# Matmul with RMS norm: one row block transposed by DMA instead of TensorE, with the products around it in a new order

## The chip, the cores and the metric

The kernel runs on one core of a Trainium2 chip. The metric is the device time in microseconds (us) of one execution, as the median of several runs. Engines are named as in the profile: PE is TensorE's matmul, PEld its weight load, DVE is VectorE, ACT is ScalarE, POOL is GpSimd, SP is SyncE (here only a queue that issues DMAs).

## The reference

All arrays are float32; a and b are 2048 x 2048, gamma has 2048 elements.

```python
x = np.matmul(a, b)
rms = np.sqrt(np.mean(x ** 2, axis=-1, keepdims=True) + eps)
return (gamma * x / rms).astype(np.float32)
```

## The kernel before

**Blocks and products.** The 16 blocks of 128 rows of a are taken in pairs, "groups" g (`NG = 8`). For a pair (rows r and r+1 of blocks) and a half j of b's columns, the 2x2 product of quarters is made by Strassen's scheme in Winograd's form: seven products m = 1..7 instead of eight, each of 8 matmuls (kp = 0..7) of 128x128 by 128x512, into one PSUM bank of 512 columns. `product_matmul(g, j, m, bank, kp, start)` (L353) issues one of them, `product` (L364) all eight. The stationary side is a quarter of transposed a (`quarter`, L321) or one of four sums of quarters (`sum_of`, `a_sums`, L331), the moving side a quarter of b or a sum (`b_diff`, `b_rest`). Sums s1, s2, s3, s4 of a feed products 5, 6, 7 and 3. A product's bank is often copied into another by ACT and the next product added on top, so the order of products and of copies is fixed by the banks: eight in all, `tbank` and `acc[0]` to `acc[6]`.

**Stages.** Blocks 0 to 3 are the head (`HB = 4`): they are computed while b arrives, the left half in `stream`, the right half in `stream_right` (L476), where blocks 0 and 1 go by plain matmuls (`head_matmul`, banks `acc[0:4]` called `plain`) and the pair of blocks 2 and 3 (`PAIR`) by products, in banks `u2`, `u4`, `p7` = `acc[4:7]`. Lines 519 to 566 end the pair and prepare blocks 4 and 5. Then `first_segment` (L611) and `segment(n)` (L642) work off the halves n = 0, 1, 2, ...: n = 0 and 1 are the left and right half of blocks 4 and 5 (group 2), n = 2 and 3 those of blocks 6 and 7, and so on. `do(n, m)` (L576) is product m of half n with the copies that follow it, `take(n, what)` (L595) brings a finished quarter into the output rows in SBUF.

**Preparing a block.** A block of a is loaded as float32 (`load_block`, L132, issued on POOL's queue), ACT sums its squares (`row_norm`, L223: two passes of 1024 columns and a root), DVE makes a scale out of it (`row_factor`, L233: four small instructions), multiplies the block by it into fp16 (`row_apply`, L244, all 2048 columns in one instruction, or two of 1024 in `prepare`, L248), and the result is transposed. Blocks 4 and 5 are transposed on TensorE: `transpose_half` (L194) is eight 128x128 transposes into one PSUM bank, and `take_transposed` (L204) copies that bank to SBUF. Blocks 6 and up use `prepare`, whose two halves go through `nc.sync.dma_start_transpose` on SP's queue.

**Finishing a row.** `square_half` and `square_right` (L278, L299) sum squares of an output row on ACT, the latter with the root; `finish(mb, order)` (L309) takes the reciprocal on DVE, multiplies each half by it and gamma (one instruction of 1024 columns) and stores it by a DMA on SP's queue. Output rows share eight slots of SBUF (`slot_of`, L256): block 4's left half goes to the slot of block 0's left half, block 5's left half to that of block 0's right half, block 4's right half to that of block 1's left half. A slot can be written only when the store of its earlier owner has read it.

**What sets the order.** The schedule is manual: every engine and every queue works strictly in the order of the program, and semaphores are put in for the data. `wait_for(src)` (L145) is a tiny POOL copy that holds POOL's queue, and so the loads behind it, until src is there. The loads of blocks 4 and 5 follow b's on the queue; those of blocks 6, 7 and 8 are three `load_block` calls at L515, L541 and L557, and block 9 comes in segment 1 behind `wait_for` on transposed block 7. Float32 blocks 4, 6, 9 share one buffer, 5 and 7 the other, block 8 has its own.

**The places that matter below**, in program order: L521 (ACT copies `u2` out), L528 (product 6 of the pair), L529 (DVE copies `u2` to `u4`), L536 and L537 (products 3 and 5 of the pair), L538 (transposes of block 4), L552 to L556 (product 4 of the pair with the transposes of block 5 in it), L558 (sums of group 2), L611 to L634 (half 0), and in `segment(1)`: `square_right(r2)`, `finish(r2, (1, 0))` and then

```python
        if j == 1:
            if first:
                a_two_sums(g)
            a_sums(g + 1, (1, 2))
```

whose sum s2 is the stationary side of `do(2, 6)`, the first product of segment 2.

Of the kernel before, what the change touches and what calls it, by code (L numbers as in the profile page):

```python
# [17 lines left out]
def kernel(  # L18
# [13 lines left out]
    nc = tc.nc  # L32
# [10 lines left out]
    HB = 4  # L43
# [224 lines left out]
    def x_chunk(mb, c):  # L268
        return x_tile(mb, c // 2)[:, (c % 2) * CH:(c % 2 + 1) * CH]
# [206 lines left out]
    def stream_right(kp):  # L476
# [11 lines left out]
        if kp == KP - 1:  # L488
            product_matmul(PAIR, 1, 7, p7, kp - 1, True)
        product_matmul(PAIR, 1, 2, u4, kp, True)  # L490
# [4 lines left out]

    for kp in range(KP):
# [22 lines left out]
    r2, r3 = HB - 2, HB - 1  # L519
    x11, x12, x21, x22 = (x_chunk(r, c) for r in (r2, r3) for c in (2, 3))  # L520
    copy_on("A")(out=x11, in_=u2)  # L521
# [6 lines left out]
    product(PAIR, 1, 6, u2, start=False)  # L528
# [5 lines left out]
    row_apply(HB + 1)  # L534
    evict(plain[2:3], "A")
    product(PAIR, 1, 3, acc[0])  # L536
    product(PAIR, 1, 5, u4, start=False)  # L537
    turned = [transpose_half(HB, h, (tbank, acc[1])[h]) for h in range(2)]  # L538
    take_transposed(HB, 0, turned[0], nc.scalar.copy)
    take_transposed(HB, 1, turned[1], nc.vector.tensor_copy)  # L540
    load_block(HB + 3)  # L541
    for r in range(HB):
        take_pre(r)
    square_right(0)
    evict(plain[3:], "A")
    square_right(1)

    def turn(h):
        view = transpose_half(HB + 1, h, (tbank, acc[2])[h])
        take_transposed(HB + 1, h, view, nc.vector.tensor_copy)  # L550

    for kp in range(KP):  # L552
        if kp == 6:
            turn(0)
        product_matmul(PAIR, 1, 4, u2, kp, False)
    turn(1)  # L556
    load_block(HB + 4)  # L557
    a_sums(G0, (3, 1, 2), False)  # L558

    def pair_ends():  # L560
        nc.scalar.copy(out=x22, in_=p7)
        nc.scalar.copy(out=x12, in_=u4)
        add(x21, u2, x22)
        add(x22, x12, x22)
        add(x12, acc[0], x12)
# [4 lines left out]
    B1, B2, B3, B7 = (acc[1], acc[0]), acc[3:5], (acc[6], acc[5]), acc[2]  # L570

# [4 lines left out]
    def do(n, m, copies=True):  # L576
# [4 lines left out]
        b1, b2, b3 = B1[n % 2], B2[n % 2], B3[n % 2]  # L581
# [13 lines left out]
    def take(n, what, engine="A"):  # L595

        x11, x12, x21, x22 = chunks(n)
        if what == 11:
            copy_on(engine)(out=x11, in_=B1[n % 2])
# [11 lines left out]
    def first_segment():  # L611
        n, g, j = 0, G0, 0
        nxt = 2 * g + 2
        do(n, 1)
        do(n, 7, False)
        finish(0, (1,))
        pair_ends()
        do(n, 2)
        row_norm(nxt)
        a_sums(g, (4,))  # L620
        finish(0, (0,))
        do(n, 6)
        do(n + 1, 1)
        prepare(nxt)
        do(n, 5)
        nc.scalar.copy(out=chunks(n)[2], in_=B7)
        take(n, 22)
        row_norm(nxt + 1)
        take(n, 11)
        finish(1)  # L630
        do(n, 4)
        take(n, 21)
        prepare(nxt + 1)
# [8 lines left out]
    def segment(n):  # L642
# [7 lines left out]
        do(n, 6)  # L650
# [25 lines left out]
        if g < G2:  # L676
            do(n, 2)
            take(n, 11)
# [233 lines left out]
```

## Time and profile before

| what | value |
|---|---|
| time, median of 3 runs | 219.43 us (219.11, 219.43, 220.07) |
| profiled execution, its time | 218.97 us |
| its span (first to last instruction) | 217.2 us |
| mean granted clock of TensorE | 0.995 |
| busy PE / DVE / ACT / POOL | 207.3 / 161.4 / 113.1 / 35.6 us |
| HBM read / written | 34.60 / 16.78 MB |
| TensorE transposes of blocks 4 and 5 (L198) | 32, from 63.19 to 66.87 us |
| DMA transposes (L253) | 20, of 128 x 1024 fp16 each |

Times are positions in the span or lengths, in us. A line of the timeline is: start, length, engine, line of the kernel, operation, what is written and read (output first), shapes, count, and in brackets the idle time of the engine just before and what ended it. Matmuls are pipelined: each is shown as 0.379 us long, but they start 0.2157 us apart (eight in 1.73 us), and it is the distance of starts that counts on PE. The chain of waits lists the pieces of work that followed on each other up to the end. "To landing" is the time from a DMA's issue to its completion.

### The profile page before, as it was taken

The numbers are of one execution on the slowest core, as the hardware profiler recorded it, in microseconds if no ns is written. First come the engines' busy times: TensorE is split into PE (matmuls) and PEld (weight loads), VectorE is DVE, ScalarE is ACT, GpSimd is POOL, SyncE is SP. The second block draws the span as 40 slices with busy tenths as digits, with TensorE's granted clock in tenths as the row PEclk, the third lists the DMA queues.
The fourth block names the chain that finished last, engine by engine and source line by source line (L and its number), as shares of the span: only waits on it lengthen the run. The fifth ranks groups of instructions, "written<-read, shape, count | busy, mean of one in ns | idle before, by whom it ended". The sixth has DMA issues, their size and how long they took to land.

```text
span 217.2 us, 2953 instructions
## 1 busy us (share of the span) xinstructions
PE 207.3 (95%) x1000; PEld 97.2 (45%) x1020; DVE 161.4 (74%) x323; ACT 113.1 (52%) x222; POOL 35.6 (16%) x74
## 2 busy tenths in 40 slices
PE   7999999999999999999999999999999999999960
PEld 3544544444455444444444444444444444444420
DVE  1128869999899997788975899399859883385771
ACT  2110002900599569498626962585777651555771
POOL 7554444334001000100021001102010000000020
PEclk9999999999999999999999999999999999999997
DMA  7999999999959798978674975499985960040455
GB/s 152 168 202 210 201 204 210 212 206 213 405 202 382 290 263 229 330 295 241 162 239 172 340 246 96 187 237 271 278 307 153 284 218 0 0 193 3 193 191 195
DMA packets 37040, 46.60 MB, mean 215 GB/s; under 512 B 22561, under 2 KB 26657, under 8 KB 35745
## 3 DMA queue, kind: packets, MB, share of 16 engines
q0 software_dynamic: 10608, 23.86, 44.8%
q1 hardware_dynamic: 26144, 22.29, 33.9%
q10 hardware_dynamic: 272, 0.26, 0.3%
q8 instruction: 8, 0.13, 0.2%
q14 instruction: 8, 0.06, 0.1%
HBM read 34.60 MB, written 16.78 MB: 237 GB/s over the span
## 4 chain that ended last, share of the span: by engine, by line
PE 68%; DMA 23%; DVE 2%; POOL 2%; issue 2%; ACT 1%; ACTq 0%; DVEq 0%; POOLq 0%
PE acc L361 61%; DMA b<-in_b_dram 18%; DMA early<-in_a_dram 5%; PE acc L400 3%; PE tbank L400 2%; POOL b L115 1%; DVE early L101 1%; PE tbank L361 1%; POOL early L119 1%; ACT a L779 1%; PE acc L198 0%; PE tbank L198 0%; DVE acc L529 0%; DVE x L101 0%; DVE b L101 0%
## 5 line engine op out<-in xcount | busy, mean ns | idle before, releaser
L361 PEld LDWEIGHTS <-s 128*128 128x128 f16 (+1 forms) x312 | 30.5, 98 | 36.9 <-DVE s L338 0.3
L275 ACT ACTIVATE sq<-x 128x1024 bf16<-128x1024 f32 (+1 forms) x33 | 33.2, 1005 | 22.6 <-DVE x L101 18.8
L409 PE MATMUL acc<-b,head_at 128*128 128x512 bf16 x171 | 42.1, 379 | 0.2
L314 DVE SCALAR_TENSOR_TENSOR x<-x,r,gamma_sb 128x1024 f32<-128x1024 f32 x28 | 35.0, 1282 | 0.5
L361 PE MATMUL acc<-b,head_at 128*128 128x512 bf16 x135 | 33.9, 379 | 0.2
L101 DVE TENSOR_TENSOR x<-acc,x 128x512 f32<-128x512 f32 x33 | 22.2, 686 | 12.5 <-PE acc L361 6.7
L361 PEld LDWEIGHTS <-head_at 128*128 128x128 f16 (+1 forms) x192 | 18.7, 98 | 22.2
L361 PE MATMUL acc<-b,at_even 128*128 128x512 bf16 x110 | 26.2, 379 | 0.1
L361 PE MATMUL acc<-early,s 128*128 128x512 bf16 x100 | 25.3, 379 | 0.2
L409 PEld LDWEIGHTS <-head_at 128*128 128x128 bf16 x176 | 16.9, 98 | 19.1
L361 PE MATMUL acc<-b,s 128*128 128x512 bf16 x102 | 24.1, 379 | 0.2
L227 ACT ACTIVATE sq<-a 128x1024 bf16<-128x1024 f32 x22 | 23.3, 1058 | 1.7 <-DMA a<-in_a_dram 1.4
L361 PEld LDWEIGHTS <-at_even 128*128 128x128 f16 x160 | 15.6, 98 | 18.6
L361 PE MATMUL acc<-t_left,s 128*128 128x512 bf16 x93 | 22.2, 379 | 0.1
L115 POOL DMA_DIRECT2D b<-in_b_dram x32 | 17.2, 540 | 20.5 <-DMA b<-in_b_dram 13.8
L448 ACT COPY x<-acc 128x512 f32<-128x512 f32 x7 | 4.0, 581 | 25.3 <-PE acc L409 25.3
L591 ACT COPY acc<-acc 128x512 f32<-128x512 f32 x12 | 6.9, 575 | 10.4 <-PE acc L361 10.4
L190 DVE COPY head_at<-tbank 128x1024 bf16<-128x1024 bf16 x7 | 4.8, 693 | 7.5 <-PE tbank L185 7.5
L296 DVE RECIPROCAL r<-rms 128x1 f32<-128x1 f32 x16 | 2.5, 159 | 9.7 <-ACT rms L291 9.7
L101 DVE TENSOR_TENSOR x<-tbank,x 128x512 f32<-128x512 f32 x9 | 6.2, 690 | 4.2 <-PE tbank L438 4.1
L782 POOL TENSOR_SCALAR x<-x,r 128x512 f32<-128x512 f32 x2 | 1.4, 688 | 47.8 <-DVE r L296 47.8
L593 ACT COPY x<-acc 128x512 f32<-128x512 f32 x10 | 5.8, 584 | 5.3 <-PE acc L361 4.9
(129 smaller groups left out, 243.4 us busy)
## 6 DMA issues: line engine op xcount, KB each, us to landing
out_dram<-x SPq DMA_DIRECT2D x29, 512.0 KB, 3.0
a<-in_a_dram POOLq DMA_DIRECT2D x9, 1024.0 KB, 6.0
b<-in_b_dram POOLq DMA_DIRECT2D x32, 256.0 KB, 9.9
a<-in_a_dram POOLq DMA_DIRECT2D x4, 512.0 KB, 9.8
early<-in_a_dram POOLq DMA_DIRECT2D x7, 256.0 KB, 10.0
gamma_sb<-in_gamma_dram POOLq DMA_DIRECT2D x2, 512.0 KB, 9.8
head_at<-in_a_dram POOLq DMA_DIRECT2D x1, 1024.0 KB, 7.8
out_dram<-x SPq DMA_DIRECT2D x3, 256.0 KB, 2.6
```

Of the source, the lines that this page charges most:

```text
L101: nc.vector.tensor_tensor(out=out, in0=in0, in1=in1, op=op)
L115: nc.gpsimd.dma_start(out=raw[j][kp][:, t, :], in_=b[lo:lo + P, j * HALF:(j + 1) * HALF])
L190: nc.vector.tensor_copy(out=head_at[:, 2 * kp:2 * kp + 2, :, :], in_=view)
L227: nc.scalar.activation(out=junk, in_=a32[mb][:, h * HALF:(h + 1) * HALF], func=ACTF.Square, scale=2.0 ** -8, accum_out=n2[:, h:h + 1])
L275: nc.scalar.activation(out=sq[:, 0:src.shape[-1]], in_=src, func=ACTF.Square, scale=inv_sqrt_n, accum_out=msq[mb][:, c:c + 1])
L314: nc.vector.scalar_tensor_tensor(out=x, in0=x, scalar=inverse_of[mb], in1=gamma_sb[:, h * HALF:(h + 1) * HALF], op0=ALU.mult, op1=ALU.mult)
L361: nc.tensor.matmul(bank, lhsT[:, kp, :], rhs, start=(start and kp == 0), stop=(kp == KP - 1), skip_group_check=not start)
L400: nc.tensor.matmul(bank, lhsT[:, k, :], rhs, start=(m in (1, 7) and k == 0), stop=(k == KQ - 1), skip_group_check=m not in (1, 7))
L409: nc.tensor.matmul(bank, head_at[:, kt, r, :], head_rhs(c, kt), start=(kt == 0), stop=(kt == KT - 1))
L448: copy_on(engine)(out=x_chunk(*g), in_=banks[g])
L591: nc.scalar.copy(out=b3, in_=b2)
L593: nc.scalar.copy(out=chunks(n)[2], in_=B7)
```

## The change

- Block 5 is no longer transposed on TensorE. DVE multiplies it into fp16 in two halves, and SP issues a DMA transpose for each. The 16 transposes and the two DVE copies out of PSUM go.
- In the last step of `stream_right`, ACT's copy of `u2` and the first four matmuls of the pair's product 6 stand ahead of the pair's product 2; the other four stay where product 6 was.
- The pair's products 3, 5, 4 are split: 3 (four matmuls), 5, 4 (six), transposes of block 4, 4 (two), 3 (two), and the last two of product 3 later in `first_segment`. The sums at the end of the pair are arranged anew; bank `acc[2]` is emptied by DVE, later, instead of ACT.
- `first_segment` takes products 1 of half 0 and half 1, then products 2 of both (half 1 in `tbank`), the rest of the pair's product 3, then 7, 6 of half 0, 6 of half 1, 5, 4. Products 1, 2 and 6 of half 1 are so taken out of `segment(1)`. `finish` of block 0's left half, the sums s4, `finish` of block 1 and `take(0, 21)` move; `prepare(7)` now stands ahead of `take(0, 21)`.
- The load of block 7 waits on POOL for block 6 to have landed; the load of block 8 waits for transposed block 6.

```diff
--- before.py
+++ after.py
@@ -486,13 +486,18 @@
         for g, kt in first:
             head_matmul(banks[g], *g, kt)
         if kp == KP - 1:
+            copy_on("A")(out=x11, in_=u2)
             product_matmul(PAIR, 1, 7, p7, kp - 1, True)
+            for k in range(4):
+                product_matmul(PAIR, 1, 6, u2, k, False)
         product_matmul(PAIR, 1, 2, u4, kp, True)
         if kp < KP - 1:
             product_matmul(PAIR, 1, 7, p7, kp - 1, True)
         for g, kt in second:
             head_matmul(banks[g], *g, kt)

+    r2, r3 = HB - 2, HB - 1
+    x11, x12, x21, x22 = (x_chunk(r, c) for r in (r2, r3) for c in (2, 3))
     for kp in range(KP):
         load_later(1)
         b_diff(1, kp)
@@ -516,58 +521,56 @@

-    r2, r3 = HB - 2, HB - 1
-    x11, x12, x21, x22 = (x_chunk(r, c) for r in (r2, r3) for c in (2, 3))
-    copy_on("A")(out=x11, in_=u2)
     product_matmul(PAIR, 1, 7, p7, KP - 1, True)
     b_rest(1, KP - 1)
     add(x11, u4, x11)
     evict(plain[:1], "A")
     row_norm(HB)
     row_norm(HB + 1)
-    product(PAIR, 1, 6, u2, start=False)
+    for kp in range(4, KP):
+        product_matmul(PAIR, 1, 6, u2, kp, False)
     nc.vector.tensor_copy(out=u4, in_=u2)
     row_factor(HB)
     row_apply(HB)
     evict(plain[1:2], "D")
     row_factor(HB + 1)
-    row_apply(HB + 1)
-    evict(plain[2:3], "A")
-    product(PAIR, 1, 3, acc[0])
-    product(PAIR, 1, 5, u4, start=False)
+
+    def part(m, bank, lo, hi, start=False):
+        for kp in range(lo, hi):
+            product_matmul(PAIR, 1, m, bank, kp, start)
+
+    part(3, acc[0], 0, 4, True)
+    part(5, u4, 0, KP)
+    part(4, u2, 0, 6)
     turned = [transpose_half(HB, h, (tbank, acc[1])[h]) for h in range(2)]
     take_transposed(HB, 0, turned[0], nc.scalar.copy)
     take_transposed(HB, 1, turned[1], nc.vector.tensor_copy)
+    src, f = a32.pop(HB + 1), factor.pop(HB + 1)
+    for h in range(2):
+        half = slice(h * HALF, (h + 1) * HALF)
+        nc.vector.tensor_scalar_mul(out=a16_first[:, half], in0=src[:, half], scalar1=f)
+        nc.sync.dma_start_transpose(at(HB + 1)[:, h * KP:(h + 1) * KP, :], a16_first[:, half])
+    wait_for(a32[HB + 2][:, 0:1])
     load_block(HB + 3)
     for r in range(HB):
         take_pre(r)
-    square_right(0)
+    part(4, u2, 6, KP)
+    part(3, acc[0], 4, 6, True)
+    nc.scalar.copy(out=x21, in_=p7)
+    nc.scalar.copy(out=x12, in_=u4)
     evict(plain[3:], "A")
-    square_right(1)
-
-    def turn(h):
-        view = transpose_half(HB + 1, h, (tbank, acc[2])[h])
-        take_transposed(HB + 1, h, view, nc.vector.tensor_copy)
-
-    for kp in range(KP):
-        if kp == 6:
-            turn(0)
-        product_matmul(PAIR, 1, 4, u2, kp, False)
-    turn(1)
-    load_block(HB + 4)
-    a_sums(G0, (3, 1, 2), False)
-
-    def pair_ends():
-        nc.scalar.copy(out=x22, in_=p7)
-        nc.scalar.copy(out=x12, in_=u4)
-        add(x21, u2, x22)
-        add(x22, x12, x22)
-        add(x12, acc[0], x12)
+    add(x22, x12, x21)
+    add(x21, u2, x21)
+    evict(plain[2:3], "D")
+    x12_pair = x12

     halves = [(g, j) for g in range(G0, NG) for j in range(2)]
     B1, B2, B3, B7 = (acc[1], acc[0]), acc[3:5], (acc[6], acc[5]), acc[2]
+
+    def b1_of(n):
+        return tbank if n == 1 else B1[n % 2]

     def chunks(n):
         g, j = halves[n]
@@ -578,7 +581,7 @@
         if n >= len(halves) or n < 0:
             return
         g, j = halves[n]
-        b1, b2, b3 = B1[n % 2], B2[n % 2], B3[n % 2]
+        b1, b2, b3 = b1_of(n), B2[n % 2], B3[n % 2]
         if g >= G2:
             b1 = b2
         product(g, j, m, {1: b1, 2: b1, 3: b3, 4: b2, 5: b3, 6: b2, 7: B7}[m],
@@ -596,7 +599,7 @@

         x11, x12, x21, x22 = chunks(n)
         if what == 11:
-            copy_on(engine)(out=x11, in_=B1[n % 2])
+            copy_on(engine)(out=x11, in_=b1_of(n))
         elif what == 12:
             copy_on(engine)(out=x12, in_=B3[n % 2])
         elif what == 22:
@@ -612,25 +615,34 @@
         n, g, j = 0, G0, 0
         nxt = 2 * g + 2
         do(n, 1)
+        square_right(0)
+        do(n + 1, 1)
+        square_right(1)
+        do(n, 2)
+        do(n + 1, 2)
+        part(3, acc[0], 6, KP, True)
+        finish(0, (1,))
+        a_sums(g, (3, 1, 2), False)
         do(n, 7, False)
-        finish(0, (1,))
-        pair_ends()
-        do(n, 2)
         row_norm(nxt)
-        a_sums(g, (4,))
+        prepare(nxt)
+        add(x12_pair, acc[0], x12_pair)
         finish(0, (0,))
         do(n, 6)
-        do(n + 1, 1)
-        prepare(nxt)
+        load_after(at(nxt)[:, KT - 1, 0:1], HB + 4)
+        product(g, 1, 6, B2[1], False)
         do(n, 5)
         nc.scalar.copy(out=chunks(n)[2], in_=B7)
+        finish(1, (0,))
+        a_sums(g, (4,))
         take(n, 22)
         row_norm(nxt + 1)
+        nc.scalar.copy(out=B3[1], in_=B2[1])
         take(n, 11)
-        finish(1)
+        prepare(nxt + 1)
         do(n, 4)
         take(n, 21)
-        prepare(nxt + 1)
+        finish(1, (1,))
         square_half(2 * g + 1, j)

     X2, W2, Y2 = tbank, B1[1], B1[0]
@@ -647,7 +659,8 @@
             block_segment(n)
             return
         first = g >= G2 and (g - G2) % 2 == 0
-        do(n, 6)
+        if n > 1:
+            do(n, 6)
         own = nxt + (g == NG - 2)
         if j == 0:
             finish(ra - 1)
@@ -673,13 +686,15 @@
                 b_two(4)
             elif not first and g > G2:
                 finish(ra - 2)
-        if g < G2:
+        if g < G2 and n > 1:
             do(n, 2)
             take(n, 11)
         if g == G2 - 1 and j == 1:
             b_two(3)
             b_two(1)
         do(n + 1, 1)
+        if n == 1:
+            take(n, 11)
         if j == 1 and g + 2 < NG:
             wait_for(at(nxt + 1)[:, KT - 1, 0:1])
             if G0 < g < NG - 3:
```

## The prediction

> **What bounds the kernel now.** I read the page's busy shares and slices first, then the chain of waits, then the timeline of the stretch that changes, then the DMA issues.
>
> ```profile
> PE 207.3 (95%) x1000; PEld 97.2 (45%) x1020; DVE 161.4 (74%) x323; ACT 113.1 (52%) x222; POOL 35.6 (16%) x74
> ...
> PE   7999999999999999999999999999999999999960
> ```
>
> PE is full from the second slice to the last but two. In the stretch of 60 to 91 us it is busy for 30.79 of 31. So only fewer PE instructions save time, and anything that makes PE wait costs its whole length. The chain of waits around the change:
>
> ```profile
> 60.02 0.70 DVE acc L529
> ...
> 61.20 0.23 DVE msq L240
> ...
> 61.47 1.89 PE acc L361 x8
> 63.35 0.45 PE tbank L198 x8
> 63.80 0.45 PE acc L198 x8
> 64.25 1.29 PE acc L361 x6
> 65.54 0.45 PE tbank L198 x8
> 65.99 0.43 PE acc L361 x2
> 66.42 0.45 PE acc L198 x8
> ```
>
> The last two L198 rows are block 5's transposes: 0.45 + 0.45 us. The DVE rows ahead say that DVE is close behind PE here. The timeline shows how close the next tight place is:
>
> ```profile
> 80.52 0.68 DVE L101 TENSOR_TENSOR x<-acc,x 128x512 f32<-128x512 f32 x1
> ...
> 81.23 1.06 ACT L275 ACTIVATE sq<-x 128x1024 bf16<-128x1024 f32 x1 [1.59 <-DVE x L101]
> ...
> 83.98 0.29 ACT L291 ACTIVATE rms<-msq,pre 128x1 f32<-128x1 f32 x1
> ...
> 84.31 0.16 DVE L296 RECIPROCAL r<-rms 128x1 f32<-128x1 f32 x1 [0.96 <-ACT rms L291]
> 84.50 2.48 DVE L314 SCALAR_TENSOR_TENSOR x<-x,r,gamma_sb 128x1024 f32<-128x1024 f32 x2
> ...
> 87.27 0.69 DVE L338 TENSOR_TENSOR head_at<-head_at 128x1024 f16<-128x1024 f16 x1 [0.28 <-DMA head_at<-a]
> 88.05 0.69 DVE L338 TENSOR_TENSOR s<-head_at 128x1024 f16<-128x1024 f16 x1
> ...
> 90.88 1.89 PE L361 MATMUL acc<-t_left,s 128*128 128x512 bf16 x8
> ```
>
> Read it as one rope: `take(0, 21)` on DVE (80.52) lets ACT square block 5's left half (81.23) and then block 2's right half; its root (83.98) lets DVE finish block 2 (84.31, 84.50); then come sums s1 and s2 of group 3 (87.27, 88.05). `do(2, 6)` needs s2, done at 88.74, and starts at 90.88: 2.1 us of slack. Last, the DMA transposes: those of block 7, beside no load (first fence), and a later pair issued 1.4 us after a load was (second).
>
> ```profile
> L253 SPq DMA_TRANSPOSE head_at<-a_half x1: 1238/1238/1238, 82.6 to 82.6; - x1
> L253 SPq DMA_TRANSPOSE head_at<-a x1: 1243/1243/1243, 84.0 to 84.0; - x1
> ...
> DMA to landing us min/median/max: 3.1/3.2/3.3
> ```
>
> ```profile
> L253 SPq DMA_TRANSPOSE at_even<-a_half x1: 1238/1238/1238, 151.3 to 151.3; - x1
> L253 SPq DMA_TRANSPOSE at_even<-a x1: 3215/3215/3215, 152.7 to 152.7; - x1
> ...
> DMA to landing us min/median/max: 5.3/5.5/5.8
> ```
>
> **The change part by part.** The sum is made against the profiled execution, 218.97 us (span 217.2 and 1.77 around it); the median of the runs is 0.46 higher, and I add the difference to the median. Positions below are in the span. A matmul takes 0.2157 us on PE, a product 1.726.
>
> *Removed:* 16 transposes, 0.90 us of PE with nothing beside them, so -0.90. The two DVE copies out of PSUM (0.69 each) go too, and DVE's one multiply of 1.28 becomes two of 0.74 (rows of L252).
>
> *Moved to the front:* four matmuls of product 6, issued from 56.72. They wait for ACT's copy of `u2`, which as before can start at 55.84 and takes 0.59: done 56.43, no wait. The four second head matmuls move 0.87 later (4 x 0.2157), and with them ACT's copy of `plain[0]` (57.35 to 58.22) and the back-to-back chain of both `row_norm` behind it: block 4's root ends at 61.37 instead of 60.50, block 5's at 63.91.
>
> *Products 3, 5, 4 of the pair:* product 5 now starts after only four matmuls, at 60.60, but needs `u4`, which DVE writes until 60.72 as before (it is bound by the end of product 6). With 0.05 to pass it on: +0.17. Product 5 then ends at 62.50, six matmuls of product 4 at 63.79. Block 4's scaled copy: root 61.37, four small DVE instructions, multiply from 62.20 to 63.48: just in time for the transposes at 63.79, cost 0; the bank of their second half is emptied by 64.07, used at 64.24. They end at 64.69; two and two matmuls fill up to 65.56. `do(0, 1)` needs that second half copied out of its own bank: DVE starts 64.89, ends 65.58, so PE starts at 65.72: +0.16.
>
> *Block 5's DMA transposes.* DVE multiplies from 65.50 and 66.28, SP issues at 66.32 and 67.76 (1.44 apart, as at 76.52 and 77.96); SP's queue is empty there. Landing 3.1 us after the second at best: 70.9. The load of block 6 is issued 0.87 later than before (64.03, as DVE frees its buffer later) and takes 5.1, so it is in flight beside them. Upper bound by the pair at 151: 67.76 + 5.8 = 73.6. I take 71.6, because here the load has a start of 2.3 us instead of 1.4. DVE is busy until 71.2 with block 0's right half (root on ACT at 69.72); s3 then ends at 72.3. `do(0, 7)`, behind four products and two matmuls, comes at 73.06. Cost 0, with 0.7 of slack; beyond a landing at 72.3 every late microsecond is one of PE.
>
> The Trainium skill (DMA: Bandwidth & Descriptors, DMA Transpose (X-bar), Alternative transpose paths) calls TensorE's way useful when the data is already on the chip, as it is here: that rule speaks against the move, and followed it would leave the 0.90 us in place and the sum at no gain. Its section Rules for kernel authors says that a transpose beside ordinary DMAs needs nothing; that is about correctness, and by it as a rule of time the landing would be 70.9 and never bind, where the row at 151 shows 5.3 to 5.8.
>
> *ACT and DVE in half 0.* ACT from 67.65 without a gap: copy, block 0's right squares and root, copy (69.63), block 1's (70.23), then `row_norm(6)` from 71.61, root done 74.28 (durations of rows 66.13 to 68.20 and 70.07 to 72.74). Before, that root was done at 72.74, and DVE never waited for it. DVE, idle from about 73.8, starts `prepare(6)` at 74.40. From there it is full: `prepare` 2.32 (75.00 to 77.32 before), the pair's add 0.61, two halves of `finish` with a reciprocal 2.59, s4 0.62, `take(0, 22)` 0.61 at 80.54, `prepare(7)` 81.15 to 83.47, and only then `take(0, 21)`, done 84.15 instead of 81.20. `do(0, 3)` needs s4 (80.64) and `take(0, 22)` (81.24), and comes at 81.70: 0.
>
> *The queues.* POOL: the load of block 7 waits for block 6 (about 69.3) and is issued near 70, landing 76.1 by the median of 6.1, used by ACT at 77.8: 0. The load of block 8 waits for transposed block 6 (80.5) and goes out near 81.2; ACT wants it after 94: 0 for itself, but it now flies beside block 7's transposes (82.67 and 84.10), so by the row at 151 those land at 89.4 instead of 87.2. Block 9's load waits for them: 90 instead of 87.8, used after 100. SP: block 0's left half is stored behind block 6's transposes, at 78.8 instead of 75.1, landing 81.7 (2.9; at worst 4.6, 83.4); ACT's `take(0, 11)` writes that slot and must be done for `do(2, 1)` at 83.43: 82.4, cost 0; at worst 84.0, cost 0.6.
>
> *The rope.* ACT squares block 5 at 84.20 (after `take(0, 21)`); block 2's root ends, with the rows' spacing, at 86.87. DVE: reciprocal 86.97, two halves of `finish` 87.16 to 89.64, s1 89.6 (block 7 landed 89.4, just no wait), s2 done 91.1. PE reaches `do(2, 6)` at 73.06 + 10 products = 90.32 and starts at 91.2: +0.9. ACT's copy into its bank ends at 90.53, less than that. Bounds: 0 if DVE's rope is 0.9 shorter than I count, 1.4 if block 7 lands half a microsecond later.
>
> After that ACT and DVE are some 1.5 us later against PE than before. In segment 2 the next needs are `take(2, 22)` ahead of `do(2, 3)` (104.4 against 105.0) and block 8's, later; segment 3 had s2 of its group 3.7 us early (111.33, used 115.05). So nothing more.
>
> Sum: -0.90 + 0.17 + 0.16 + 0.90 = +0.33. 218.97 becomes 219.3, the median 219.43 becomes 219.8.
>
> **The rivals.** I take 0.5% (1.1 us) as about what a measurement of this kernel can tell from no change.
>
> *Cover holds.* DVE reaches s2 a microsecond earlier, since its idle gaps (about 0.6 at 73.8, 1.5 before 86.97) are thinner than I count, and the whole saving stays less small waits: -0.90 + 0.33 = -0.57, 218.9; without these two 218.5. For it: before, DVE was busy for only 0.35 and 0.66 us of the two from 83 to 85. Against: `take(0, 21)` is put behind `prepare(7)`, 2.3 us, by order alone.
>
> *Block 5 lands late (slower).* The load of block 6, and block 7's behind it, slow the transposes as at 151. Landing at 73.1 (5.3): s3 at 73.8, `do(0, 7)` 0.8 late; DVE's `prepare(6)` 0.7 late, so the rope again costs 0.8: -0.90 + 0.33 + 0.8 + 0.8 = +1.0, 220.5. Landing at 73.6: 1.35 and 0.8, +1.6, 221.0. It decides from a landing of about 72.3. For it: the second transpose at 152.7 was held in issue for 3.2 us. Against: the load's start here is earlier.
>
> *Store of block 0 late.* `take(0, 11)` at 84.0: +0.6 on `do(2, 1)`, of which the rope takes most back, since PE is then late anyway: 219.8 to 220.2.
>
> **How the numbers follow.** Forecast 0.43 (219.4 to 220.2), cover holds 0.19, block 5 late 0.25, store late 0.07, other 0.06. The likeliest is 219.8. The range goes from cover held (218.6) to block 5 at its upper bound (221.0), which leaves about 0.15 out. Faster than 218.3 would need more than the 0.90 that is removed: two thirds of "other", 0.04. Slower than 220.5: four fifths of the late case (0.20), half of the late store and the rest of "other" (0.05): 0.25. The same: 0.71.
>
> **What would show it.** Right: 16 instead of 32 at L198's place; PE idle near 60.7 and 65.6 for 0.2 each; DVE waiting for ACT's norm near 74; a weight load waiting for DVE's s near 91 for about 0.9; block 7's transposes landing in over 5 us. Wrong: a weight load waiting for s near 73 (late case), an unbroken PE at 91 (cover holds), or a wait on PE past 100 us, where I count none.

## The result and the profile after

The changed kernel takes 220.63 us, the median of 15 runs (219.84 to 221.95), beside 219.20 us for the kernel before on the same chip (15 runs). The ratio is 1.0062, 95% interval 1.0044 to 1.0079: slower by a little over half a per cent, where the forecast was 219.8 with the range 218.6 to 221.0. The profiled execution of it is the slowest of the 15: 221.95 us, span 220.2.

The page of the changed kernel, busy shares and slices:

```profile
PE 207.7 (94%) x985; PEld 95.6 (43%) x1004; DVE 161.0 (73%) x323; ACT 112.8 (51%) x221; POOL 36.6 (17%) x76
...
PE   7999999999999999899999999899999999999960
```

The unbroken row of nines has two eights, in the slices at 88 to 94 us and at 138 to 143 us. The weight load that precedes each matmul shows what was waited for. Its waits in the kernel before, then in the changed one:

```profile
PEld L361 <- DVE s L338: 0.3, 1, 0.3
```

```profile
PEld L361 <- DVE s L338: 2.9, 3, 1.3
...
PEld L361 <- DMA head_at<-a_half: 0.8, 1, 0.8
...
PEld L361 <- DMA head_at<-a: 0.3, 1, 0.3
```

The columns are total, number of waits and longest. One wait for a sum s has become three, and two waits for transposed blocks have appeared. Now the timeline of the changed kernel where the transposes went:

```profile
61.41 1.89 PE L361 MATMUL acc<-b,head_at 128*128 128x512 bf16 x7
...
64.43 0.61 PE L198 MATMUL tbank<-identity_h,x 128*128 128x128 f16 x8
...
64.88 0.61 PE L198 MATMUL acc<-identity_h,x 128*128 128x128 f16 x8
...
66.27 1.89 PE L361 MATMUL acc<-b,at_even 128*128 128x512 bf16 x8
...
66.91 3.84 SPq L552 DMA_TRANSPOSE at_even<-a_first x2
...
72.96 0.69 DVE L338 TENSOR_TENSOR s<-at_even 128x1024 f16<-128x1024 f16 x1 [1.24 <-DMA at_even<-a_first]
...
73.71 1.47 PE L361 MATMUL acc<-t_left,s 128*128 128x512 bf16 x6
```

16 transposes instead of 32. Product 5 of the pair (61.41) starts 0.09 late and `do(0, 1)` (66.27) 0.08, by the distance of starts; DVE waits 1.24 for block 5's DMA transposes, and `do(0, 7)` starts 0.11 late. The rope and the first product of segment 2 in the changed kernel:

```profile
81.92 0.53 POOL L137 DMA_DIRECT2D head_at<-in_a_dram  x1 [0.28 <-issue]
...
84.49 1.06 ACT L275 ACTIVATE sq<-x 128x1024 bf16<-128x1024 f32 x1 [1.26 <-DVE x L101]
84.55 3.79 SPq L253 DMA_TRANSPOSE head_at<-a  x1
...
87.39 2.48 DVE L314 SCALAR_TENSOR_TENSOR x<-x,r,gamma_sb 128x1024 f32<-128x1024 f32 x2
...
90.52 0.69 DVE L338 TENSOR_TENSOR head_at<-head_at 128x1024 f16<-128x1024 f16 x1 [0.65 <-DMA head_at<-a]
...
91.24 0.69 DVE L338 TENSOR_TENSOR s<-head_at 128x1024 f16<-128x1024 f16 x1
...
91.99 1.90 PE L361 MATMUL acc<-t_left,s 128*128 128x512 bf16 x7 [0.85 <-DVE s L338]
```

Load 8 goes out on POOL at 81.92, block 7's second transpose on SP at 84.55, and SP is held for 3.79 us by it. DVE has finished block 2 at 89.87 and then stands for 0.65 until that transpose has landed. PE is idle for 0.85 in the row; by the distance of starts it lost 1.00. The landing of block 7's pair, by its DMA rows (before: 3.1 to 3.3):

```profile
DMA to landing us min/median/max: 5.9/6.1/6.4
```

Further on, where the prediction had nothing:

```profile
118.50 0.53 POOL L137 DMA_DIRECT2D a<-in_a_dram  x1 [0.37 <-ACT sq L275]
...
123.26 3.27 SPq L253 DMA_TRANSPOSE head_at<-a_half  x1
...
126.69 2.54 SPq L253 DMA_TRANSPOSE head_at<-a  x1
...
130.44 0.55 PEld L361 LDWEIGHTS <-head_at 128*128 128x128 f16 x4 [0.78 <-DMA head_at<-a_half]
130.49 0.75 DVE L252 TENSOR_SCALAR a_half<-a,s 128x1024 f16<-128x1024 f32 x1 [1.15 <-DMA head_at<-a_half]
...
138.16 1.41 PEld L361 LDWEIGHTS <-s 128*128 128x128 f16 x8 [1.14 <-DVE s L338]
```

Load 11 is issued at 118.50 (before: 116.30) and block 10's transposes at 123.26 and 126.69 land after 7.1 and 4.5 us (before: issued at 122.1 and 123.6, landing after 3.4 and 3.1). PE waits at 130.44 for the transposed block. DVE too: its next `prepare` writes the one fp16 buffer that the late transpose is still reading, so block 11 is late as well, and PE waits again at 138. Between load 11 and these transposes SP issues two stores of finished rows. Their landing in the changed kernel, then in the kernel before:

```profile
L317 SPq DMA_DIRECT2D out_dram<-x x2: 332/332/332, 120.2 to 121.4; - x2
...
DMA to landing us min/median/max: 8.0/8.0/8.0
```

```profile
L317 SPq DMA_DIRECT2D out_dram<-x x2: 332/332/333, 119.1 to 120.3; - x2
...
DMA to landing us min/median/max: 3.6/3.8/3.9
```

In the changed kernel load 11 lands at 125.59, these stores at 128.15 and 129.39, and the first transpose, behind them on the same queue, at 130.40.

**Where the 3.0 us of span come from.** Up to the end of `stream_right` both kernels execute the same program, yet the same matmul (`acc<-b,head_at`, product 1, in the last step) starts at 55.42 before and at 56.14 here: 0.72, which I put down to the arrival of the first loads. This place differed by up to 1.6 us between the executions profiled in this study, with and without the change alike, and belongs to no kernel. So I compare two more stretches: the *body*, from that matmul to the start of the last product (`tbank<-early,s`, 204.84 before, 207.46 here), and the *end*, from the issue of the last store to the end of the span (unrounded, where the views print it to 0.1 us). The body is 1.90 longer, the end 0.35 (4.45 before, 4.80 here); 0.72 + 1.90 + 0.35 = 2.97. In the body the waits by the distance of starts are 0.09 + 0.08 + 0.11 + 1.00 + 0.45 + 0.81, and 0.22 at 150.49: 2.76, less 0.88 for the transposes, 1.88.

### The profile page after: what moved, and what is told of

Its sections match the earlier page's. It is cut to its first block, busy times and chain, and to the rows that moved or that the text cites. A ratio compares the mean times of both kernels' runs of the same rounds, so it can differ in the third digit from the quotient of the medians.

```text
span 220.2 us, 2927 instructions
## 1 busy us (share of the span) xinstructions
PE 207.7 (94%) x985; PEld 95.6 (43%) x1004; DVE 161.0 (73%) x323; ACT 112.8 (51%) x221; POOL 36.6 (17%) x76
## 4 chain that ended last, share of the span: by engine, by line
PE 67%; DMA 19%; ACT 4%; DVE 3%; issue 2%; POOL 2%; SPq 0%; POOLq 0%; DVEq 0%; ACTq 0%
PE acc L361 49%; PE acc L409 11%; DMA early<-in_a_dram 5%; DMA b<-in_b_dram 4%; DMA head_at<-a 4%; DMA head_at<-a_half 3%; PE tbank L361 2%; DMA a<-in_a_dram 2%; ACT sq L227 2%; PE acc L400 2%; PE tbank L400 1%; POOL b L115 1%; PE tbank L438 1%; PE tbank L185 1%; POOL early L119 1%
## 5 line engine op out<-in xcount | busy, mean ns | idle before, releaser
L361 PE MATMUL acc<-b,s 128*128 128x512 bf16 x104 | 24.7, 379 | 0.0
L361 PE MATMUL acc<-b,at_even 128*128 128x512 bf16 x93 | 22.4, 379 | 0.1
L448 ACT COPY x<-acc 128x512 f32<-128x512 f32 x6 | 3.4, 592 | 27.0 <-PE acc L409 27.0
L594 ACT COPY acc<-acc 128x512 f32<-128x512 f32 x11 | 6.3, 575 | 12.9 <-PE acc L361 12.9
L596 ACT COPY x<-acc 128x512 f32<-128x512 f32 x10 | 5.8, 584 | 5.0 <-PE acc L361 4.6
```

Source lines behind the costliest of these rows:

```text
L361: nc.tensor.matmul(bank, lhsT[:, kp, :], rhs, start=(start and kp == 0), stop=(kp == KP - 1), skip_group_check=not start)
L448: copy_on(engine)(out=x_chunk(*g), in_=banks[g])
L594: nc.scalar.copy(out=b3, in_=b2)
```

## The experiments

All ratios are to the kernel before on the same chip. "Body" and "end" are from the profiled execution, as just defined, with the body as its difference to that of the kernel before.

| run | ratio, 95% interval | body | end |
|---|---|---|---|
| before | 1 | 0 | 4.45 |
| the change, first profile | 1.0062, 1.0044 to 1.0079 | +1.90 | 4.80 |
| e8_changed_again | 1.0044, 1.0026 to 1.0061 | +0.40 | 4.80 |
| e7_no_turn | 0.9976, 0.9965 to 0.9987 | -0.47 | 4.44 |
| e1_front_only | 1.0034, 1.0020 to 1.0048 | +0.60 | 4.46 |
| e2_load8_after_t7 | 1.0093, 1.0069 to 1.0117 | +1.52 | 4.80 |
| e3_load11_no_wait | 1.0056, 1.0036 to 1.0076 | +0.99 | 4.80 |
| e4_load8_and_load11 | 1.0020, 1.0007 to 1.0034 | +0.23 | 4.81 |
| e5_take21_first | 1.0037, 1.0021 to 1.0053 | +0.47 | 4.81 |
| e6_loads_and_take21 | 1.0099, 1.0082 to 1.0116 | +0.78 | 4.79 |
| e9_before_two_more | 1.0021, 1.0009 to 1.0033 | -0.01 | 4.80 |
| e10_loads_lanes | 1.0002, 0.9978 to 1.0026 | -0.08 | 4.42 |
| e11_load8_early_lanes | 1.0283, 1.0256 to 1.0310 | +5.49 | 4.45 |
| e12_load8_early_take21 | 1.0271, 1.0252 to 1.0290 | +6.20 | 4.43 |

My theory after the result: the transposes' time is saved; most of the wait before `do(2, 6)` is load 8 flying beside block 7's transposes; and the waits at 130 and 138 are the same thing once more, load 11 beside block 10's. The rivals: the wait is the rope itself (`take(0, 21)` behind `prepare(7)`), or the front reorder costs what I put at nothing.

### The change again, and the removal alone

The changed kernel was run once more, unaltered.

> The changed kernel once more, as it is. Its first profile was of its slowest execution (221.95 us, median 220.63): PE was 0.72 us late there before the change begins, and block 10's first transpose met a load and cost two waits, 0.45 us at 130.4 and 0.82 at 138.2 (by the distance of starts). Theory A (the meeting belongs to the order of POOL's queue): this profile too shows the waits near 130 and 138 with the transpose landing after more than 5 us, and PE's wait before product 6 of half 2 of about 1.0 us; ratio 1.006. Rival B (the meeting is an accident of one execution): PE waits near 91 us only, block 10's first transpose lands in under 4 us, ratio still 1.005 to 1.006, and something else has to hold the difference.

220.14 us, ratio 1.0044. Its waits for s and for the transposes, and the POOL issue of load 11:

```profile
PEld L361 <- DVE s L338: 1.8, 2, 1.1
```

```profile
117.92 0.53 POOL L137 DMA_DIRECT2D a<-in_a_dram  x1 [0.37 <-issue]
```

The waits at 130 and 138 are not there: the collision of load 11 with block 10's transposes belongs to some executions and not to others. Here load 11 was out 5.2 us ahead of the first transpose (123.16), and the pair landed after 5.5 and 4.5 us; in the first profile it was 4.8 ahead, and 7.1 and 4.5; before, 5.8 ahead, and 3.4 and 3.1. The body is 0.09 + 0.08 + 0.32 (at `do(0, 7)`) + 0.79 (at `do(2, 6)`) - 0.88 = +0.40.

For the price of the 16 transposes, the kernel before was run without them. Its short edit is in the function `turn` of the kernel before:

```diff
-        view = transpose_half(HB + 1, h, (tbank, acc[2])[h])
+        view = tbank.bitcast(FP16).rearrange("p (g m) -> p g m", m=P)
```

> The kernel before without the 16 TensorE transposes of block 5: the DVE copies stay and take block 4's transposed half from the other bank, so block 5's rows are computed from block 4's data. Everything else is as before. It measures the most that taking these transposes off PE can bring by itself. Theory A: they lie on PE with nothing beside them, 16 x 0.056 = -0.90 us, ratio 0.996. Rival B (DVE or a DMA is the bound a little later and takes the time back): 0 to -0.3 us, ratio 0.999 to 1.000, and a new wait of PE shows between 68 and 91 us.

218.46 us, 0.9976. Not 0.90 but 0.47 us came out of the body, since a wait takes the rest back:

```profile
67.97 1.90 PE L361 MATMUL acc<-t_left,s 128*128 128x512 bf16 x8 [0.25 <-DVE s L338]
```

With `do(0, 1)` earlier, DVE's sum is late by 0.41 (distance of starts). -0.88 + 0.41 = -0.47. So even free of cost, the removal could bring 0.5 us unless DVE's work was moved too. In this run DVE's two copies out of PSUM stay (they take block 4's transposed half), and the sum stands behind them; the change takes them out as well, and has its sum wait for the DMA transposes instead.

### The front reorder alone

The kernel before, with the copy of `u2` and four matmuls of product 6 put forward as in the change, and nothing else:

```diff
         if kp == KP - 1:
+            copy_on("A")(out=x11, in_=u2)
             product_matmul(PAIR, 1, 7, p7, kp - 1, True)
+            for k in range(4):
+                product_matmul(PAIR, 1, 6, u2, k, False)
...
-    copy_on("A")(out=x11, in_=u2)
...
-    product(PAIR, 1, 6, u2, start=False)
+    for kp in range(4, KP):
+        product_matmul(PAIR, 1, 6, u2, kp, False)
```

> The kernel before with one part of the change alone: ACT's copy of u2 and four matmuls of the pair's product 6 stand ahead of the pair's product 2 in the last step of stream_right. In the profiled execution of the changed kernel PE is 0.72 us later than before already at the first head matmuls of that step (54.85 for 54.13), ahead of anything the change touches. Theory A (chance from one execution to the next, the reorder costs nothing): ratio to before 1.000, within 0.002. Rival B (the new order or what it does to the code slows the head): +0.7 us, ratio 1.003, and PE at the first matmul of product 2 late by that much in this profile too.

219.74 us, 1.0034. That is the rival's number (1.003), but not for its reason: the head ends 0.24 later than before, within what it differs by between executions, and the rest comes behind it. In the profile of this run ACT's chain is what moved:

```profile
58.45 0.59 ACT L448 COPY x<-acc 128x512 f32<-128x512 f32 x1 [1.79 <-PE acc L409]
...
61.30 0.30 ACT L230 ACTIVATE norm<-n 128x1 f32<-128x1 f32 x1
...
63.67 0.62 PE L198 MATMUL tbank<-identity_h,x 128*128 128x128 f16 x8
...
66.22 0.62 PE L198 MATMUL tbank<-identity_h,a_first 128*128 128x128 f16 x8
```

Less the later head (0.24), ACT's copy of `plain[0]` and block 4's root are 0.86 later than before (57.35 and 60.20), as I had worked out; and here nothing stands ahead of the transposes to cover it. PE waits 0.24 for block 4's and 0.22 for block 5's fp16 data, and 0.14 between the two halves of block 4; the body is 0.60 longer. In the change, products 5 and 4 stand there, and the same 0.86 costs nothing. My zero for this part was right only together with the other parts.

### Load 8 and load 11

In the change, load 8 waits on POOL for transposed block 6 and is issued just ahead of block 7's transposes. This run issues it after them, with load 9:

```diff
-        load_after(at(nxt)[:, KT - 1, 0:1], HB + 4)
...
             wait_for(at(nxt + 1)[:, KT - 1, 0:1])
+            if g == G0:
+                load_block(HB + 4)
```

> The changed kernel, but block 8 is loaded after block 7's DMA transposes have landed, just ahead of block 9, instead of after block 6's. So no load flies beside the transposes of block 7. Theory A (in the changed kernel the wait before product 6 of half 2, 0.85 us, is 0.65 of load beside transposes and 0.2 of DVE's order): the second transpose lands 3.1 to 3.3 us after its issue instead of 5.9, the wait falls to 0.2, the time by about 0.65 us: ratio to before 1.003; if the later waits at 130 and 138 us are an echo of the same lateness they go too and the ratio is 0.999. Rival B (it is the order on DVE, take(0, 21) behind prepare(7)): the wait stays 0.8 with DVE waiting for ACT's root and not for the DMA, ratio 1.006.

The landing of block 7's transposes in this run:

```profile
DMA to landing us min/median/max: 3.2/3.3/3.3
```

They land after 3.2 to 3.3 us instead of 5.9 to 6.4, and the wait at `do(2, 6)` falls from 1.00 (0.79 in the second profile) to 0.25. So 0.5 to 0.75 of it is load 8. But the time is 221.2 us, 1.0093: waits of 0.77 at 129.26, 0.75 at 136.93 and 0.33 at 149.35 stay. Load 11 is issued at 117.42 in this run, and block 10's transposes meet it again.

Load 11 waits on POOL for block 10 to have landed. Without that wait:

```diff
                 load_block(nxt + 2)
-                wait_for(a32[nxt + 2][:, 0:1])
+                if g > G0 + 1:
+                    wait_for(a32[nxt + 2][:, 0:1])
```

> The changed kernel, but the load of block 11 no longer waits on POOL for block 10 to have landed (group 3's segment alone; the later groups keep that wait). In the changed kernel the first transpose of block 10, issued at 123.26, lands after 7.1 us, 3.4 before; the load of block 11 was issued at 118.50. Theory A (that load, made late by the chain of waits on POOL's queue, flies beside block 10's transposes): issued some 5 us earlier it is done by then, block 10's first transpose lands in 3.4 us, both PE waits at 130.4 (0.29) and 138.2 (0.65) go, time -0.94 us, ratio to before 1.002. Rival B (stores of the rows or SP's own queue delay the transpose): landing stays near 7 us, ratio 1.006.

220.15 us, 1.0056. No wait at 130 or 138 is left, and `do(2, 6)` still waits 1.09: the two are separate. Both edits together:

> The changed kernel with both moves of loads: block 8 after block 7's transposes have landed, block 11 without the wait for block 10. Theory A (the loss is two meetings of a load with transposes, the rest is small waits): no wait over 0.3 us on PE between 56 and 140 us; -0.90 + 0.3 + 0.25 = -0.35 against before, ratio 0.998 to 0.999. Rival B (the lateness of ACT and DVE finds another place): some other PE wait takes it back, ratio 1.003 or more.

219.48 us, 1.0020. Waits 0.08 + 0.09 + 0.54 (`do(0, 7)`) + 0.25 (`do(2, 6)`) + 0.15 (at 105.65) - 0.88 = +0.23, which is the body. By the ratios, 0.9 of the change's 1.36 us (0.62% of 219.2, the first series) or 0.5 of its 0.96 (0.44%, the second) came from these two loads.

### Is it the order of take(0, 21)?

```diff
-        prepare(nxt + 1)
         do(n, 4)
         take(n, 21)
+        prepare(nxt + 1)
```

> The changed kernel with one exchange: take(0, 21) stands ahead of prepare(7) on DVE again, as in the kernel before. Theory A (load 8 beside block 7's transposes sets the wait before product 6 of half 2): take(0, 21) must wait for product 4, so prepare(7) and the transposes go out about 1 us later, land later than 90.5, and PE's wait stays 1.0 us or grows to 1.7: ratio 1.006 to 1.009. Rival B (the rope from take(0, 21) over ACT's squares and finish of block 2 to the sums): squares and finish come 1 us earlier, the wait falls below 0.3, ratio 1.003.

220.1 us, 1.0037 [1.0021, 1.0053]. DVE in this run:

```profile
86.25 2.48 DVE L314 SCALAR_TENSOR_TENSOR x<-x,r,gamma_sb 128x1024 f32<-128x1024 f32 x2
...
89.74 0.69 DVE L338 TENSOR_TENSOR head_at<-head_at 128x1024 f16<-128x1024 f16 x1 [1.01 <-DMA head_at<-a]
...
91.21 1.90 PE L361 MATMUL acc<-t_left,s 128*128 128x512 bf16 x8 [0.51 <-DVE s L338]
```

DVE's `finish` begins 1.14 earlier than in the change (86.25 against 87.39; 0.30 when the heads, 0.84 apart, are allowed for), and DVE just waits longer, 1.01 instead of 0.65, for block 7's transposes, since these are prepared later. The wait at `do(2, 6)` is 0.67. So the last wait there is the landing, not the order that the prediction blamed.

All three edits at once:

> The changed kernel with all three: both moves of loads, and take(0, 21) ahead of prepare(7). Theory A: without a load beside them block 7's transposes land 3.2 us after an issue near 85.5, about 88.7, and the sums are ready before PE needs them: the last 0.25 us before product 6 of half 2 go too, ratio 0.997 to 0.998, the best of all. Rival B (prepare(7) made later by the exchange costs as much as the rope gains): as with the two loads alone, ratio 0.998 to 0.999.

221.39 us, 1.0099: worse. The wait at 91 is gone, and another has come:

```profile
90.09 0.53 POOL L137 DMA_DIRECT2D head_at<-in_a_dram  x1
...
106.29 1.89 PE L361 MATMUL acc<-b,s 128*128 128x512 bf16 x8 [1.24 <-DVE x L101]
```

Load 8, behind transposes that are themselves later, goes out at 90.09, 8 us later than in the change. DVE then stands for 2.95 us at 100.20, waiting for ACT's norm of the block, and what DVE owes PE behind it, a quarter of the output at 106.29, is 1.40 late. In e4, where load 8 goes out at 89.08, the wait at this place is 0.15: here PE comes to it 0.70 earlier, as measured from the head, and DVE is 0.55 later. That load 8 is the reason is argued from these rows; it was not tried alone.

### The 0.35 us at the end

Every kernel with the change and its stores in one piece ends 4.79 to 4.81 us after its last store is issued, before it was 4.45. Among the records of SP, the last thing in the span is a row of semaphore checks, some 0.06 us each. In the kernel before the one on the last store stands ninth of ten; in the changed one it stands third, and seven follow when the store has landed. The change issues two more DMAs on SP's queue (block 5's transposes). To see whether this is the cause, the kernel before was given two more, and nothing else:

```diff
-            nc.sync.dma_start(out=rows(mb, h * HALF, (h + 1) * HALF), in_=x)
+            if mb in (8,):
+                for c in range(2):
+                    lo = h * HALF + c * CH
+                    nc.sync.dma_start(out=rows(mb, lo, lo + CH), in_=x[:, c * CH:(c + 1) * CH])
+            else:
+                nc.sync.dma_start(out=rows(mb, h * HALF, (h + 1) * HALF), in_=x)
```

> The kernel before, with each of the two stores of block 8 issued as two DMAs of 512 columns: two more DMAs on SP's queue, as many as the change adds, and nothing else. Theory (the two additional DMAs shift the last store's place among those that SP checks one by one at the end): the stretch from the landing of the last store to the end of the span is 1.3 us instead of 0.95, and the ratio to the kernel before 1.0016 (0.35 of 219). Rival (the 0.35 us at the end of the changed kernel comes from something else of its order): the stretch stays 0.95 and the ratio is 1.000. The smaller stores land in the middle of segment 5, where nobody waits for them: 0 under both.

219.41 us, 1.0021 [1.0009, 1.0033]. The last store in this run and its span, and those of the kernel before:

```profile
core 0 of [0], span 218.9 us
...
214.08 0.33 SPq L877 DMA_DIRECT2D out_dram<-a  x1
```

```profile
core 0 of [0], span 217.2 us
...
212.75 0.33 SPq L872 DMA_DIRECT2D out_dram<-a  x1
```

The end is 4.80 instead of 4.45, the body unchanged (-0.01). The cost has nothing to do with what the two DMAs do. And with six more on top of the change's two, in the kernel of e4 (the same edit with `mb in (8, 9, 10)`):

> The kernel of run e4 (the changed one with load 8 behind block 7's transposes and load 11 without its wait), with the stores of blocks 8, 9 and 10 issued as two DMAs each: six more on SP's queue, eight more than the kernel before. Theory (what counts is the number of SP's DMAs modulo eight): the stretch after the last store's landing is back at 0.95 us, and the time 0.35 us below that of e4, ratio about 1.0004. Rival (every additional DMA lengthens the end, or none does): the stretch is 1.3 us or longer, ratio 1.002 or more.

219.15 us, ratio 1.0002 [0.9978, 1.0026]. The end is back:

```profile
core 0 of [0], span 216.9 us
...
212.52 0.33 SPq L894 DMA_DIRECT2D out_dram<-a  x1
```

4.42. Eight more DMAs cost nothing at the end where two cost 0.35. The place in the row goes by the count modulo eight, as far as three counts (0, 2, 8) can show. The body is -0.08 (waits of 0.16, 0.08, 0.30 and 0.25, less 0.88). This is the best form of the change that I found. It is level with the kernel before, not better.

### Load 8 still earlier

```diff
-        load_after(at(nxt)[:, KT - 1, 0:1], HB + 4)
+        load_after(a32[nxt + 1][:, 0:1], HB + 4)
```

This on the change, with load 11 free of its wait and the six split stores (by which its line numbers are up to 5 higher):

> The changed kernel with three edits: the load of block 8 is issued as soon as that of block 7 has landed (near 77 us instead of 82), so that most of it is over when block 7's transposes are issued at 84.5; the load of block 11 without its wait; the same six split stores. Theory (the wait before product 6 of half 2 is made by load 8 beside block 7's transposes): that wait falls from 0.8 to 1.0 us to 0.3 or less, none is left at 130 and 138, the end is 0.35 shorter: -0.5 to -0.9 for what is removed (run e7 and the 16 transposes), +0.2 of small waits, +0.3, ratio 0.998 to 1.000, median near 218.8. Rival (load 8 then disturbs block 6's transposes at 77 to 82 instead, which product 1 and 2 of half 2 or the sum s4 need): a new wait of 0.5 us or more between 80 and 90, ratio 1.002 or more.

225.14 us, 1.0283: far outside both. The rows of this run:

```profile
79.08 0.53 POOL L137 DMA_DIRECT2D head_at<-in_a_dram  x1
...
79.59 1.25 SPq L322 DMA_DIRECT2D out_dram<-x  x2
...
87.28 0.58 ACT L607 COPY x<-acc 128x512 f32<-128x512 f32 x1 [5.80 <-DMA out_dram<-x]
...
87.91 2.55 PE L366 MATMUL acc<-b,head_at 128*128 128x512 bf16 x8 [3.69 <-ACT x L607]
...
90.25 2.96 PE L366 MATMUL acc<-early,s 128*128 128x512 bf16 x8
```

What held PE was not block 6's transposes (issued 76.52 and 78.29; the second took 5.5 us to land instead of 3.1, but was there at 83.78) but the store of block 0's left half behind them. Issued at 79.59, half a microsecond after the load, it took 7.6 us to land instead of 3.0. `take(0, 11)` on ACT may not write that slot before, and `do(2, 1)` may not start before `take(0, 11)`. This is my third rival, "store of block 0 late", with a price of 3.85 instead of 0.6. And there is a second price. The windows of the same run (columns: window, busy time of PE, PEld, DVE, ACT, POOL, granted clock, DMA share, GB/s):

```profile
84.00:88.00 4.00, 0.31 (x3) 0.09 (x1) 1.70 (x2) 0.72 (x2) 0.00 (x0) 1.00 1.01 384
88.00:89.00 1.00, 1.00 (x6) 0.41 (x6) 0.00 (x0) 0.97 (x3) 0.00 (x0) 1.00 1.24 261
89.00:92.40 3.40, 3.40 (x10) 1.16 (x9) 1.92 (x3) 3.30 (x7) 0.71 (x2) 0.50 0.73 228
92.40:95.00 2.60, 2.60 (x14) 1.19 (x13) 2.46 (x4) 2.57 (x6) 0.00 (x0) 1.00 0.86 217
```

After the stall the granted clock is 0.50 for 3.4 us, from 89.0 to 92.4. The two products behind it take 2.34 and 2.80 us instead of 1.73: 1.69 more. 3.85 + 1.69 and the small waits at 60 to 74, less 0.88, make the 5.5. The Trainium skill (TensorE: Matmul & The Clock Gate, Part 1) says that the clock drops to half after an idle window of about 3.4 us and then needs about as long of steady work. The 3.85 of idle time, the 0.43 us between starts in the slow stretch (weight loads from 89.40 to 92.39) and its length agree. No stall of 1.4 us or less in the other runs brought the clock down in this way.

The same with `take(0, 21)` first:

> As the run before it, with take(0, 21) ahead of prepare(7) as well. Theory (the order of take(0, 21) and prepare(7) on DVE makes the rest of the wait before product 6 of half 2, some 0.25 us): that rest goes, ratio 0.001 below the run before it. Rival (prepare(7) is then later by 0.7 us, and with it block 7's transposes, the sums that need them and block 8 behind them, as in run e6): ratio the same or higher, with a wait at 91 or near 106.

225.2 us, 1.0271: the same stall (3.88), so it says nothing about `take(0, 21)`. Here the granted clock is 0.50 from 86.1 to 92.9, and the products at 87.51 and 90.88 take 3.37 and 2.74 us: 2.66 more instead of 1.69. The last matmul ahead of the stall ends at 83.79, so in this run the clock fell after 2.3 us of idle time, not 3.4.

## Why the prediction was nearly right, and where not

The chief number, +0.33 against the profiled execution, stands beside a body of +0.40 in the second profile of the changed kernel. The medians, 220.14 and 220.63, are 0.3 and 0.8 us above the forecast of 219.8, and inside its range. The size of the move was not foreseen: +0.96 and +1.36 us by the ratios, where the sum had +0.33. That the range holds the result is partly luck, since what makes up the difference, the end and block 10, was nowhere in the sum. By its steps:

- **"16 transposes, -0.90".** In nine profiles (the first, e2 to e8, e10) the body is the sum of the waits less 0.88, within 0.03. Right. That it isn't all to be had, I had not seen: e7 gives 0.47.
- **"+0.17" and "+0.16", product 5 and `do(0, 1)`.** Both waits are there: 0.09 to 0.30 for product 5 (0.09 in both profiles of the change), 0.08 for `do(0, 1)`. Right in place, half the size together.
- **"Front: cost 0".** Right in the change, by the cover of products 5 and 4; 0.60 without it (e1).
- **"Block 5's DMA transposes: landing 71.6, cost 0".** Mis-sized. Less the 0.72 of the head, DVE was let go at 72.24, close to my limit of 72.3, and `do(0, 7)` paid 0.06 to 0.54 (0.11 and 0.32 in the two profiles of the change). The load of block 6 beside them (issued at 64.64, the transposes at 66.91) makes the landing 4.6 to 5.2 us (4.8 to 5.4 in the second profile) rather than the 3.8 that I took; the row at 151 (5.3 to 5.8) was the better neighbour than the one without a load.
- **"The rope: +0.9" at `do(2, 6)`.** 1.00 and 0.79, at 91.27 on the time axis of before, where I had 91.2. But the mechanism was only half mine. I had DVE's `finish` end at 89.64 and block 7 land at 89.4, "just no wait". Measured on that axis: 89.15 and about 89.8. The transposes bind, by 0.65, and e2, e4 (0.25 left) and e5 (no use in moving `take(0, 21)`) show it. The right total was luck, two errors of opposite sign: the rope 0.5 too long, the landing 0.4 too short (5.3 taken, 5.9 to 6.4 measured).
- **"After that ... So nothing more."** This is the step that failed. I looked for waits of PE on ACT and DVE past 100 us and not at the chain on POOL: load 10 waits for transposed block 9, and load 11 for block 10 to have landed. Load 9 is issued at 91.19 instead of 87.82, block 9's transposes at 106.99 instead of 105.28, load 10 at 112.30 instead of 110.58, load 11 at 118.50 instead of 116.30 (0.72 of each is the head). That load 8 beside block 7's transposes starts this is not shown: in e2, where block 7 lands as before, load 11 is 1.15 late on the axis of before, against 0.99 and 1.48 in the two profiles of the change. Common to the three are block 9's transposes, 1.0 late, behind the lateness of ACT and DVE that I had written down. Block 10's transposes, due at nearly the old time (122.5 against 122.1, less the head), then meet load 11 and the stores behind it: +0.45 and +0.81 in the first profile, nothing in the second. I had written down such a collision for block 7 and did not follow the queue one round further. My sign for being wrong, "a wait on PE past 100 us", is what came in the first profile.
- **The end, +0.35.** Not in the sum at all. I had counted the two more DMAs on SP as free since its queue was empty; the queue was, and the end of the program was not. e9 and e10 show it.

Forecast +0.33, plus 0.35 at the end, plus 0 to 1.26 for block 10 (0.45 + 0.81), reaches from +0.7 to +1.9; the two series gave +0.96 and +1.36. Of the rivals, "cover holds" needed s2 earlier, which e4 has in part, and its 0.5 went into `do(0, 7)` and the end. "Block 5 lands late" is partly in the result, its first price (0.1 to 0.5 at `do(0, 7)`). "Store late" did not happen: ACT was let go by the store at 82.65, which is 81.93 on the axis of before, where I had 82.4. e11 showed how near it was.

On the rule of the Trainium skill that I weighed (DMA: Bandwidth & Descriptors, Rules for kernel authors: a transpose beside ordinary DMAs needs nothing): as a rule of time it does not hold here. Block 7's transposes, of 128 x 1024, landed after 3.1 to 3.3 us before and after 5.7 to 6.4 in the two profiles of the change, behind a load issued 1.2 to 2.6 us ahead. But a load in flight does not settle it: in the changed kernel the pair issued at 146.45 and 148.11 landed after 3.0 and 3.1 us with a load in flight from 142.96 to 148.20, and in the kernel before the pair at 170.36 and 171.78, behind two stores and with no load in flight, after 4.9 and 4.3. The page's other remark (DMA Transpose (X-bar), Alternative transpose paths), that TensorE's way is useful when the data is on the chip, agrees with the outcome: the best form of the move is worth 1.0002.

What stays open: what decides whether block 10 collides in an execution. The distance between load 11 and the transposes (4.8 and 5.2 us) differs by half a microsecond between the two profiles, no more than what the wait at `do(2, 6)` and the arrival of loads vary by; no run varied it alone. Of the other two forms of the change that keep load 11's wait, e2 has the collision at a distance of 4.3 and e5 has none at 5.3; of the six profiles without that wait (e3, e4, e6, e10 to e12) none has it. Open too is whether load 11 slows the transposes directly or by way of the two stores ahead of them, which took 8.0 us instead of 3.6 to 3.9: no run parts the two.

## What to carry to other kernels

Work that is moved from an engine to a DMA queue is not paid for by the engine any more, but by every transfer that now flies beside another; price a DMA by the row that has the same neighbours in flight, and follow each delayed load round its queue until its lateness is absorbed. A tuned schedule gives back only as much of a removed piece as the next engine is ahead (0.47 of 0.90 here), and a load moved to "a free place" may be beside something tighter than what it left (e6, e11). Compare bodies between two fixed matmuls rather than spans when the arrival of the first loads varies by more than the effect.

## What the runs showed of the hardware that I had not expected

- The end of the program depends on how many DMAs the queue of SP has issued: 4.44 to 4.46 us after the last store's issue with the count of the kernel before, 4.79 to 4.81 with 2 more, 4.42 to 4.45 with 8 more.
- A store of 512 KB on SP's queue took 7.6 us to land instead of 3.0 when a load of 1 MB had been issued on POOL's 0.5 us ahead of it.
- A stall of PE of 3.85 us is paid for one and a half times: the granted clock of 0.50 afterwards added 1.69 (2.66 after a stall of 3.88 in e12).
- The same program's head ended at places up to 1.6 us apart (55.19 to 56.76) in the executions profiled.
